# Keeping four weight tiles for the second token tile, and sending its last 512 columns out by ScalarE and an adding transfer

## The chip, the core and the metric

The kernel runs on one core of a Trainium2 chip. Its engines are TensorE (PE, with its weight loads as PEld), VectorE (DVE), ScalarE (ACT), GpSimd (POOL) and SyncE (SP). SP and POOL also issue transfers between memory and the on-chip buffers, which 16 DMA engines carry out. The metric is the device time in microseconds (us), as the median of several runs.

## The reference

One layer of a hybrid encoder on 256 tokens of width 2048, all in float32. A mixer (two kinds of attention and a recurrence) comes first; its output is normalised and added to x. Then comes the part that matters here:

```python
hdn = jnp.square(jax.nn.relu(_rms_norm(x, norm_mlp_pre[l]) @ w_mlp_up[l]))
x = x + _rms_norm(hdn @ w_mlp_down[l], norm_mlp_post[l])
```

with w_mlp_up of 2048 x 8192 and w_mlp_down of 8192 x 2048. `_rms_norm` divides a token's row by the root of the mean of its squares and multiplies by a gain for each column. The last product, its norm and the addition to x end the kernel.

## The kernel before

Each float32 weight is used as the sum of two rounded parts: ACT copies a weight tile of 128 x 1024 into the upper part (`whi`, L158), DVE subtracts to get the lower part (`wlo`, L159), and TensorE multiplies with both. The 256 tokens are two token tiles of 128 (`tt` = 0, 1). Weight tiles come from memory one by one: `wraw` (L143) issues a load on SP's queue into one of three `raw` buffers, `wsplit` (L151) splits it, and `wnext` (L162) keeps one tile ahead. The parts go to three buffers each of `whi` and `wlo`, unless the list `homes` (L149) names another place for that tile; `raw2` (L1185) makes such places, of which there are six.

The residual x stays in memory (`xs`) while the large products run, and is fetched back into `x1[0]` and `x1[1]` near the end. The sums of the last product are gathered in `ys[0]` and `ys[1]`, 128 x 2048 each.

The end of the kernel is the loop at L1600. It takes the last eight 128-row blocks of `hdn` and multiplies them by four groups g of 512 columns; each group takes four weight tiles. `tok` (L192) does one group. For most weight tiles it multiplies for both token tiles (12 matmuls, L220); the last `lag` tiles are kept: they are multiplied for token tile 0 first (six matmuls each, L204), then token tile 0 is given out, then the kept tiles are multiplied for token tile 1. `lag` is 1, and 3 for g = 3.

In the group g = 2 the residual is fetched back (L1608), in four transfers of 512 KB on SP's queue. For each token tile, DVE adds the product to `ys` (L1611), ACT squares and sums (L1612), and DVE multiplies by the gain (L1615). For g = 3 the row's factor follows: `rstd_of` (L1158) takes the mean on DVE (L1166) and raises it to the power -0.5 on POOL (L1167). `final` (L1623) then scales a piece of columns, adds the residual (DVE, L1625) and issues its transfer to the output (SP, L1626). For token tile 0, two pieces of 512 columns are done so and two more after the last addition of token tile 1 (L1638, L1639); for token tile 1 it is three pieces of 512 columns and two of 256.

A planner arranges the instructions of each engine, and of each queue, when the program is built. It goes by when their inputs and buffers come free in its own reckoning, and then by program order. The matmuls of this part are planned like the rest. `issue_after` puts an instruction behind another on the same engine. On the chip each engine and each queue runs its list in order: an instruction that waits holds up all behind it. POOL can issue transfers that add to what is at their destination (`accum_op`, L1439); before, these add weight tiles on the chip.

Of the kernel before, what the change touches and what calls it, by code (L numbers as in the profile page):

```python
# [12 lines left out]
AF = mybir.ActivationFunctionType  # L13
ALU = mybir.AluOpType
# [36 lines left out]
def hybrid_block(ctx, tc, xt, x, gains, params, consts, lora, gup, wst, out):  # L51
    nc = tc.nc
    V, A, G, PE = nc.vector, nc.scalar, nc.gpsimd, nc.tensor
# [11 lines left out]
    def nm(s):  # L65
        uid[0] += 1
        return f"{s}_{uid[0]}"

    def gps():
        return pg.tile([128, 512], F32, tag="gps", name=nm("gps"), bufs=4)  # L70
# [54 lines left out]
    def tick(us):  # L125

        clock[0] += us
        while any([step(th) for th in list(threads)]):
            pass
# [19 lines left out]
    homes = []  # L149
# [12 lines left out]
    def wnext():  # L162

        while len(wq) < 1 + AHEAD and (order or wpos[0] < wst.shape[0]):
            wsplit(wraw(order.pop(0) if order else None))
            if side:
                side.pop(0)()
        return wq.pop(0)
# [15 lines left out]
    def unit(pks):  # L184

        ps = gps()
        for h in range(2):
            hi, lo = wnext()
            gemm(ps, hi, lo, pks[8 * h:8 * h + 8], h == 0, h == 1, tick)
        return ps  # L190

    def tok(pks, lag=1):  # L192


        ps = [gps(), gps()]
        n = len(pks)
        kept = []

        def prod(hl, k0, tt):
            for w, parts in ((hl[0], (0, T)), (hl[1], (0,))):  # L200
                for k in (k0, k0 + 1):
                    for part in parts:
                        c = part + tt * 128
                        PE.matmul(ps[tt], pks[k][:, c:c + 128], w[:, (k - k0) * 512:(k - k0) * 512 + 512],  # L204
                                  start=k == 0 and part == 0 and w is hl[0], stop=w is hl[1] and k == n - 1)
                    if k == k0 + 1 or w is hl[0]:
                        tick(2 * US)

        for k0 in range(0, n, 2):
            hl = wnext()  # L210
            if k0 >= n - 2 * lag:
                prod(hl, k0, 0)
                kept.append((hl, k0))
                continue
            for w, parts in ((hl[0], (0, T)), (hl[1], (0,))):
                for k in (k0, k0 + 1):
                    for tt in range(2):
                        for part in parts:
                            c = part + tt * 128
                            PE.matmul(ps[tt], pks[k][:, c:c + 128], w[:, (k - k0) * 512:(k - k0) * 512 + 512],  # L220
                                      start=k == 0 and part == 0 and w is hl[0], stop=False)
                        tick(len(parts) * US)
        yield ps[0]
        for hl, k0 in kept:
            prod(hl, k0, 1)
        yield ps[1]
# [91 lines left out]
    w = {}  # L318
# [92 lines left out]
    for h in range(8):  # L411
        ps = qb[h] if h < 3 else unit(upk)
# [641 lines left out]
    for s in ("q", "k"):  # L1054
        lst = []
        for h in range(4):
            ps = unit(upk)
# [12 lines left out]
    for hf in range(2):  # L1070
        for s, mo in (("k", MU_K), ("r", MU_R), ("v", MU_V)):
            for p in range(4 * hf, 4 * hf + 4):
                ps = unit(upk)
# [84 lines left out]
    def rstd_of(ss, eps, sums):  # L1158

        if sums is None:  # L1160
            sums = cpool.tile([128, 1], F32, name=nm("ssum"))
            V.tensor_reduce(sums, ss[:, 0:3], AX.X, ALU.add)
            V.tensor_scalar(sums, sums, 1.0 / D, eps, ALU.mult, ALU.add)
            return sums
        r = cpool.tile([128, 1], F32, name=nm("rs"))
        V.tensor_scalar(r, ss[:, 3:4], 1.0 / D, sums, ALU.mult, ALU.add)  # L1166
        G.tensor_tensor(r, r, cst[:, 2:3], ALU.pow)  # L1167
        return r

    g2, loads = gain(0, [fm().rearrange("p a b -> p (a b)")[:, 0:512] for _ in range(4)])  # L1170
    x1 = [p2.tile([128, D], F32, tag="x1", name=nm("x1"), bufs=2) for _ in range(2)]
    for c in range(0, D, 512):
        for tt in range(2):
            loads.append(lambda tt=tt, c=c: nc.sync.dma_start(out=x1[tt][:, c:c + 512],
                                                              in_=x[tt * 128:tt * 128 + 128, c:c + 512]))
# [3 lines left out]
    def junk():  # L1179
        return p2.tile([128, 512], F32, tag="junk", name=nm("junk"), bufs=2)  # L1180
# [10 lines left out]
    for g in range(4):  # L1191
# [4 lines left out]
        for tt, ps in enumerate(tok(mpk, 5 if g == 3 else 1)):  # L1196
            def gained():
                return V.tensor_tensor(mg[tt][:, gs], ps, g2[g], ALU.mult)
# [148 lines left out]
    ys = []  # L1347
    hid, fmh, fml, hp = {}, {}, {}, {}
# [176 lines left out]
    for j in range(2):  # L1525
        up(j)
        ps, post = heads[j]
# [69 lines left out]
    hp = [hp[k] for k in range(FIRST[4], FIRST[4] + SIZES[4])]  # L1597
    g4, loads = gain(1, [pk() for _ in range(4)])
    side.extend(loads)
    for g in range(4):  # L1600
        gs = slice(512 * g, 512 * g + 512)
        if g == 2:
            assert not threads
            spare.clear()
            x1 = [p2.tile([128, D], F32, tag="x1", name=nm("x1"), bufs=2) for _ in range(2)]
            for tt in range(2):
                for c in (0, 1024):
                    nc.sync.dma_start(out=x1[tt][:, c:c + 1024], in_=xs[tt][:, c:c + 1024])  # L1608
        for tt, ps in enumerate(tok(hp, 3 if g == 3 else 1)):
            yv = ys[tt][:, gs]  # L1610
            added = V.tensor_tensor(yv, yv, ps, ALU.add)  # L1611
            A.activation(junk(), yv, AF.Square, accum_out=ss4[:, tt, g:g + 1])  # L1612

            def gained():
                V.tensor_tensor(yv, yv, g4[g], ALU.mult)  # L1615

            if g < 3:
                gained()
                if g == 2:
                    sum4.append(rstd_of(ss4[:, tt, :], eps4[tt], None))  # L1620
                continue

            def final(c, w):  # L1623
                cs = slice(c, c + w)
                V.scalar_tensor_tensor(x1[tt][:, cs], ys[tt][:, cs], r4, x1[tt][:, cs], ALU.mult, ALU.add)  # L1625
                nc.sync.dma_start(out=out[tt * 128:tt * 128 + 128, cs], in_=x1[tt][:, cs])  # L1626

            if tt == 0:
                r4 = rstd_of(ss4[:, 0, :], None, sum4[0])
                gained()  # L1630
                final(0, 512)
                final(512, 512)
                r40 = r4
                continue
            with tc.issue_after(added.ins):
                for c in (1024, 1536):
                    cs = slice(c, c + 512)
                    V.scalar_tensor_tensor(x1[0][:, cs], ys[0][:, cs], r40, x1[0][:, cs], ALU.mult, ALU.add)  # L1638
                    nc.sync.dma_start(out=out[0:128, cs], in_=x1[0][:, cs])  # L1639
            r4 = rstd_of(ss4[:, 1, :], None, sum4[1])  # L1640
            gained()
            for c, w in ((0, 512), (512, 512), (1024, 512), (1536, 256), (1792, 256)):
                final(c, w)


# [123 lines left out]
```

## Time and profile before

| | us |
|---|---|
| median of 3 runs | 1495.91 (1495.70 to 1497.13) |
| the profiled execution, its time | 1496.71 |
| the profiled execution, its span | 1494.9 |
| TensorE busy | 1480.5 |
| TensorE's granted clock, mean | 0.998 |

The span runs from the first to the last instruction. Times in the views are microseconds from the start of the span. Busy time of one instruction includes what overlaps with the next one on the same engine, so that matmuls of 0.39 us follow each other more closely than that. The column of a wait names what ended last before the instruction could start.

### The profile page before, as it was taken

The page shows a single profiled execution, that of the slowest core. Times are in us where ns is not written, and L with a number is a line of the kernel's source. Part 1 is how long each engine was busy: PE and PEld are TensorE (multiplying, and loading weights), DVE is VectorE, ACT ScalarE, POOL GpSimd, SP SyncE. Part 2 cuts the span into 40 slices and gives each one's busy share as a digit, 9 for nine tenths or more (in the row PEclk, how much of TensorE's full clock was granted, in tenths as well). Part 3 has the DMA queues.
Part 4 walks back from the last instruction along what each step waited for, and adds up shares of the span by engine and source line. Part 5 has one row for each costly group of instructions (what it writes and reads, how often), then busy time and mean ns, then how long its engine had stood idle before and what let it go on. Part 6 is the DMA issues. An engine that isn't in the chain of part 4 may idle for free.

```text
span 1494.9 us, 22860 instructions
## 1 busy us (share of the span) xinstructions
PE 1480.5 (99%) x8429; PEld 1250.2 (84%) x8429; DVE 1214.0 (81%) x1688; ACT 933.9 (62%) x1396; POOL 91.3 (6%) x160
## 2 busy tenths in 40 slices
PE   9999999999999999999999999999999999999997
PEld 7888888888778888788888888888888888888885
DVE  7576677899679798567646788999899999899986
ACT  7465666664576554574445767776766677677653
POOL 0021000100001100000000000000000000000000
PEclk9999999999999999999999999999999999999999
DMA  7545545445544556445755768888888888889874
GB/s 274 187 152 189 169 169 179 171 165 192 175 150 167 179 172 201 152 148 197 267 197 202 277 213 246 258 257 257 242 254 245 262 240 249 258 246 280 261 248 155
DMA packets 107759, 317.70 MB, mean 213 GB/s; under 512 B 10752, under 2 KB 14976, under 8 KB 107392
## 3 DMA queue, kind: packets, MB, share of 16 engines
q1 hardware_dynamic: 94400, 283.34, 55.2%
q0 software_dynamic: 8064, 29.36, 10.5%
q10 hardware_dynamic: 5184, 3.54, 0.8%
q8 instruction: 66, 1.08, 0.3%
q14 instruction: 45, 0.37, 0.1%
HBM read 282.65 MB, written 4.19 MB: 192 GB/s over the span
## 4 chain that ended last, share of the span: by engine, by line
PE 96%; DVE 1%; ACT 1%; issue 1%; POOL 0%; DMA 0%; POOLq 0%; DVEq 0%; ACTq 0%; SPq 0%
PE gps L220 28%; PE gps L174 22%; PE gps L178 13%; PE gps L204 7%; PE mps L1479 3%; PE mps L1477 3%; PE mps L1478 3%; PE gps L1479 3%; PE gps L1477 2%; PE gps L1478 2%; PE gps L182 2%; PE gps L335 1%; PE mps L790 1%; DVE wlo L159 0%; PE gps L1236 0%
## 5 line engine op out<-in xcount | busy, mean ns | idle before, releaser
L159 DVE TENSOR_TENSOR wlo<-raw,whi 128x1024 fp32r<-128x1024 f32 x497 | 602.3, 1220 | 154.0 <-ACT whi L158 139.5
L158 ACT ACTIVATE whi<-raw 128x1024 fp32r<-128x1024 f32 x497 | 522.7, 1056 | 247.9 <-PE gps L220 85.4
L174 PE MATMUL gps<-pk,whi 128*128 128x512 f32 x1336 | 336.6, 391 | 0.4 <-ACT whi L158 0.4
L174 PEld LDWEIGHTS gps<-pk,whi 128*128 128x128 f32 x1336 | 247.3, 188 | 48.9 <-ACT whi L158 0.6
L220 PE MATMUL gps<-whi,pk 128*128 128x512 f32 x1136 | 286.0, 391 | 0.0
L220 PEld LDWEIGHTS gps<-whi,pk 128*128 128x128 f32 x1136 | 211.5, 188 | 44.0
L178 PEld LDWEIGHTS gps<-pk,wlo 128*128 128x128 f32 x1424 | 194.1, 190 | 14.1 <-DVE wlo L159 0.3
L178 PE MATMUL gps<-pk,wlo 128*128 128x256 f32 x1424 | 199.2, 282 | 0.0
L220 PE MATMUL gps<-wlo,pk 128*128 128x512 f32 x568 | 155.2, 392 | 0.0
L220 PEld LDWEIGHTS gps<-wlo,pk 128*128 128x128 f32 x568 | 105.6, 188 | 21.9
L1340 DVE TENSOR_TENSOR sp<-raw,sp 128x1024 fp32r<-128x1024 f32 x67 | 81.7, 1219 | 3.4 <-ACT sp L1339 3.1
L1368 ACT ACTIVATE sp<-gps 128x512 f32<-128x512 f32 x52 | 31.1, 598 | 80.0 <-PE gps L182 80.0
L1339 ACT ACTIVATE sp<-raw 128x1024 fp32r<-128x1024 f32 x67 | 70.6, 1054 | 14.0 <-PE mps L1478 4.9
L204 PE MATMUL gps<-whi,pk 128*128 128x512 f32 x256 | 68.9, 390 | 0.0
L1477 PE MATMUL mps<-whi,fm 128*128 128x512 f32 x168 | 66.2, 394 | 0.0
L1478 PE MATMUL mps<-whi,fm 128*128 128x512 f32 x168 | 65.8, 392 | 0.0
L1479 PE MATMUL mps<-wlo,fm 128*128 128x512 f32 x168 | 65.6, 391 | 0.1
L1439 POOL DMA_DIRECT2D raw<-raw x40 | 34.9, 874 | 426.2 <-DVE raw L1436 110.1
L204 PEld LDWEIGHTS gps<-whi,pk 128*128 128x128 f32 x256 | 47.7, 188 | 9.9
L1479 PE MATMUL gps<-wlo,fm 128*128 128x512 f32 x126 | 49.3, 391 | 0.5 <-DVE wlo L159 0.5
L1477 PE MATMUL gps<-whi,fm 128*128 128x512 f32 x126 | 49.2, 391 | 0.0
L1436 DVE TENSOR_TENSOR raw<-raw,raw 128x1024 f32<-128x1024 f32 x40 | 48.8, 1219 | 0.4
(393 smaller groups left out, 2007.2 us busy)
## 6 DMA issues: line engine op xcount, KB each, us to landing
raw<-in_wst_dram SPq DMA_DIRECT2D x499, 512.0 KB, 4.4
raw<-raw POOLq DMA_DIRECT2D x40, 512.0 KB, 7.1
sp<-in_wst_dram SPq DMA_DIRECT2D x16, 512.0 KB, 5.7
raw<-sp POOLq DMA_DIRECT2D x8, 512.0 KB, 6.4
sp<-raw POOLq DMA_DIRECT2D x8, 512.0 KB, 7.3
x<-in_x_dram SPq DMA_DIRECT2D x8, 256.0 KB, 5.6
xs<-x SPq DMA_DIRECT2D x2, 1024.0 KB, 4.6
x<-xs SPq DMA_DIRECT2D x4, 512.0 KB, 6.9
```

Of the source, the lines that this page charges most:

```text
L158: A.activation(hi, raw, AF.Copy)
L159: V.tensor_tensor(lo, raw, hi.bitcast(F32), ALU.subtract)
L174: PE.matmul(ps, hi[:, i * 128:i * 128 + 128], pks[i], start=first and i == 0, stop=False)
L178: PE.matmul(ps[:, 0:T], lo[:, i * 128:i * 128 + 128], pks[i][:, 0:T], start=False, stop=False)
L204: PE.matmul(ps[tt], pks[k][:, c:c + 128], w[:, (k - k0) * 512:(k - k0) * 512 + 512], start=k == 0 and part == 0 and w is hl[0], stop=w is ...
L220: PE.matmul(ps[tt], pks[k][:, c:c + 128], w[:, (k - k0) * 512:(k - k0) * 512 + 512], start=k == 0 and part == 0 and w is hl[0], stop=False)
L1339: A.activation(hi, raw, AF.Copy)
L1340: V.tensor_tensor(lo, raw, hi.bitcast(F32), ALU.subtract)
L1436: V.tensor_tensor(x, x, z, ALU.add)
L1477: PE.matmul(Q[f], p, w, start=d == 0 and i == 0, stop=False)
L1478: PE.matmul(Q[f], pl, w, start=False, stop=False)
L1479: PE.matmul(Q[f], p, wl, start=False, stop=d == nd - 1 and i == 1)
```

## The change

For g = 3, `tok` keeps all four weight tiles (`lag` 4), and the parts of the fourth go to a pair of `raw2` buffers. Token tile 0 does three pieces of 512 columns before, and one after, the last addition of token tile 1. For token tile 1 the columns 1536 to 2047 are taken from DVE and SP: in the block of g = 2 the residual of these columns is copied from `x1[1]` to the output in memory (a transfer of 256 KB on SP's queue), and at the end ACT multiplies `ys[1]` there by the row's factor into `x1[1]`, and POOL issues a transfer that adds this to the output in memory. DVE and SP do the other columns in pieces of 512, 512, 256 and 256.

```diff
                 for c in (0, 1024):
                     nc.sync.dma_start(out=x1[tt][:, c:c + 1024], in_=xs[tt][:, c:c + 1024])
-        for tt, ps in enumerate(tok(hp, 3 if g == 3 else 1)):
+            nc.sync.dma_start(out=out[128:256, 1536:2048], in_=x1[1][:, 1536:2048])
+        if g == 3:
+            homes[:] = [None, None, raw2]
+        for tt, ps in enumerate(tok(hp, 4 if g == 3 else 1)):
...
                 r4 = rstd_of(ss4[:, 0, :], None, sum4[0])
                 gained()
-                final(0, 512)
-                final(512, 512)
+                for c in (0, 512, 1024):
+                    final(c, 512)
                 r40 = r4
                 continue
             with tc.issue_after(added.ins):
-                for c in (1024, 1536):
+                for c in (1536,):
                     cs = slice(c, c + 512)
...
             r4 = rstd_of(ss4[:, 1, :], None, sum4[1])
             gained()
-            for c, w in ((0, 512), (512, 512), (1024, 512), (1536, 256), (1792, 256)):
+            part = x1[1][:, 1536:2048]
+            A.activation(part, ys[1][:, 1536:2048], AF.Copy, scale=r4)
+            G.dma_start(out=out[128:256, 1536:2048], in_=part, accum_op=ALU.add)
+            for c, w in ((0, 512), (512, 512), (1024, 256), (1280, 256)):
                 final(c, w)
```

## Rows read from the trace of the kernel before

**Rows 1.** The page, busy us of each engine, share of the span, instructions.
```profile
PE 1480.5 (99%) x8429; PEld 1250.2 (84%) x8429; DVE 1214.0 (81%) x1688; ACT 933.9 (62%) x1396; POOL 91.3 (6%) x160
```

**Rows 2.** Chain of waits from 1440 on, pieces of g = 3: start, us, what.
```profile
1473.97 2.72 PE gps L220 x12
1476.69 4.09 PE gps L204 x18
```

**Rows 3.** DVE in order of time: start, us, engine, line, output<-inputs, count, idle before.
```profile
1483.61 1.42 DVE L1625 SCALAR_TENSOR_TENSOR x<-y,rs,x 128x512 f32<-128x512 f32 x2 [0.46 <-POOL rs L1167]
1484.95 0.68 DVE L1611 TENSOR_TENSOR y<-y,gps 128x512 f32<-128x512 f32 x1
1485.54 1.41 DVE L1638 SCALAR_TENSOR_TENSOR x<-y,rs,x 128x512 f32<-128x512 f32 x2
1486.87 0.20 DVE L1166 TENSOR_SCALAR rs<-ss,ssum 128x1 f32<-128x1 f32 x1
...
1488.11 2.87 DVE L1625 SCALAR_TENSOR_TENSOR x<-y,rs,x 128x512 f32<-128x512 f32 x5 [0.44 <-POOL rs L1167]
```

**Rows 4.** ACT and POOL in order of time, the same stretch.
```profile
1485.72 0.63 ACT L1612 ACTIVATE junk<-y 128x512 f32<-128x512 f32 x1 [3.41 <-DVE y L1611]
1486.25 0.19 ACT L1612 ACTIVATION_READ_ACCUMULATOR junk<-y 128x1 f32 x1
...
1487.15 0.92 POOL L1167 TENSOR_TENSOR rs<-rs,cst 128x1 f32<-128x1 f32 x1 [3.57 <-DVE rs L1166]
```

**Rows 5.** Line L1626: landing of all seven writes; then the last one alone.
```profile
DMA to landing us min/median/max: 2.5/2.8/3.2
...
L1626 SPq DMA_DIRECT2D out_dram<-x x1: 411/411/411, 1491.1 to 1491.1; - x1
DMA to landing us min/median/max: 2.9/2.9/2.9
```

**Rows 6.** DVE and ACT in order of time: splits of the last two weight tiles.
```profile
1475.28 1.22 DVE L159 TENSOR_TENSOR wlo<-raw,whi 128x1024 fp32r<-128x1024 f32 x1
1475.87 1.06 ACT L158 ACTIVATE whi<-raw 128x1024 fp32r<-128x1024 f32 x1 [0.21 <-ACT junk L1612]
1477.20 1.21 DVE L159 TENSOR_TENSOR wlo<-raw,whi 128x1024 fp32r<-128x1024 f32 x1
```

**Rows 7.** Groups by line and form: count | busy us, mean ns | idle before.
```profile
L1091 ACT ACTIVATE th<-gps,rt 128x512 f32<-128x512 f32 x22 | 14.8, 679 | 7.5 <-PE gps L204 5.9 <-DVE wlo L159 1.5
```

**Rows 8.** Line L1439, adding transfers: landing of all 56; then the last alone.
```profile
DMA to landing us min/median/max: 4.5/7.0/11.0
...
DMA to landing us min/median/max: 5.1/5.1/5.1
```

**Rows 9.** DMA queues (packets, MB, share) from 1431 to 1438.5; 1488.6 to 1494.9; 1486.2 to 1488.6.
```profile
q0 software_dynamic: 144, 0.52, 35.3%
...
q1 hardware_dynamic: 734, 1.06, 54.0%
...
q1 hardware_dynamic: 365, 0.67, 80.3%
```

**Rows 10.** SP's queue and ACT in time; landing of L1608, of L145; SP's longest wait.
```profile
1441.50 2.08 SPq L1608 DMA_DIRECT2D x<-xs  x2
1444.94 0.33 SPq L145 DMA_DIRECT2D raw<-in_wst_dram  x1
1449.00 1.55 SPq L145 DMA_DIRECT2D raw<-in_wst_dram  x2
...
1453.42 1.06 ACT L158 ACTIVATE whi<-raw 128x1024 fp32r<-128x1024 f32 x1 [0.69 <-DMA raw<-in_wst_dram]
...
DMA to landing us min/median/max: 4.0/6.9/8.3
...
DMA to landing us min/median/max: 3.1/4.4/7.1
...
SPq L1608 <- DMA raw<-sp: 5.6, 1, 5.6
```

## The prediction

> **What bounds the kernel now.** I read the page's busy times first, then the chain of waits, then the last stretch in order of time, then the queues. TensorE is busy for 1480.5 us, 99% of the span [rows 1]. So whatever the change does beside a running TensorE is worth nothing, unless it makes TensorE wait. Only the stretch after the last matmul can become shorter.
>
> In the chain of waits the last column group (g = 3) starts at 1473.97: 12 matmuls that serve both token tiles (2.72 us), then 18 for the first token tile, 18 for the second [rows 2]. One matmul steps 2.72/12 = 0.227 us. The first token tile is complete at 1476.69 + 4.09 = 1480.78, the second at 1473.97 + 48 x 0.227 = 1484.85. From there to the end of the span, 1494.9, there are 10.05 us without a matmul: this tail is all that the change works on directly.
>
> The tail in order of time [rows 3, 4]: DVE adds the last product (L1611, 1484.95), ACT squares and sums (L1612, 1485.72, its sum is read out until 1486.25 + 0.19 = 1486.44), DVE makes the mean (L1166) only at 1486.87, POOL raises it to the power -0.5 (L1167, 1487.15), DVE scales and adds five pieces (L1625, from 1488.11), and SP sends each to memory. The last transfer is issued at 1491.1 and lands 2.9 us later [rows 5], at 1494.0; 0.9 us of closing follow. Two things stand out. For the first token tile the same chain took 1483.61 - 1480.78 = 2.83 us from its last matmul to its first scaled piece [rows 2, 3]; for the second it took 1488.11 - 1484.85 = 3.26. The difference, 0.43 us, is DVE still doing two pieces of the first tile (L1638, 1485.54 to 1486.95) when ACT's sum is there at 1486.44. And the five pieces and their issue take 1491.1 - 1488.11 = 3.0 us, one engine doing them all.
>
> **The change, part by part.** (1) *Four weight tiles kept instead of three.* The number of matmuls is the same, 48, so TensorE still ends at 1484.85, but the first 24 are all for the first token tile: it is complete at 1473.97 + 5.44 = 1479.41, that is 1.37 us sooner. In return the weight tiles are wanted sooner, the third at 1476.69 instead of 1478.05, the fourth at 1478.05 (upper parts) and 1478.05 + 4 x 0.227 = 1478.96 (lower parts) instead of 1479.41 and later. By the rows their splits are there in time: the third's lower part is done at 1475.28 + 1.22 = 1476.50, the fourth's upper part at 1475.87 + 1.06 = 1476.93, and its lower part at 1477.20 + 1.21 = 1478.41, 0.55 us ahead [rows 6]. The fourth goes to a pair of other buffers (raw2), so that it no longer waits for the first to be used up. Cost taken: 0. If DVE orders something else ahead, one 512-column operation (0.68 us) costs 0.1 us of TensorE.
>
> (2) *Three pieces of the first tile ahead of the last product, one behind.* They can start at 1479.41 + 2.83 = 1482.24 and take 3 x 0.71 = 2.1 us of DVE [rows 3], until 1484.4, before the last product at 1484.85. Behind it one piece is left, until about 1486.3, ahead of ACT's sum. So the 0.43 us are gained: the first scaled piece of the second tile comes at 1484.85 + 2.83 = 1487.68.
>
> (3) *The last 512 columns leave DVE and SP.* DVE and SP then do 512, 512, 256 and 256 columns. One 512 step is 0.67 us (half of 1.41, less the overlap; 2.87 for all five) [rows 3], so SP's last issue comes at 1491.1 - 0.43 - 0.67 = 1490.0, and with the same 2.9 us of landing and 0.9 of closing this branch ends at 1493.8: **1.1 us** ahead of before. This is the most that the tail can give.
>
> (4) *The new branch.* ACT scales 512 columns with a factor for each partition: 0.63 us by L1612, 0.68 by the nearest row with such a factor, L1091 [rows 4, 7]. It starts at 1487.68 like DVE, since both wait for the same power, so POOL can issue the adding transfer at about 1488.4. POOL has nothing else to do. What the transfer takes to land, the trace of before shows only for others: 512 KB into SBUF, 4.5 / 7.0 / 11.0 us (least, median, most), and 5.1 for the last one, which ran nearly alone at its end [rows 8]. Here it is 256 KB into memory. Its packets took 35.3% of 16 engines in 7.5 us [rows 9], 42 engine-us or 2.65 us on all 16 engines; half the bytes save 1.3 us, so alone it would land in 3.8. That is the lower end, and 7.0, the median of the full size among other traffic, the upper; 11.0 is a tail. I take 4.9: the 3.8, 0.7 for the writes beside it (the tail's own writes stretch from 2.5 to 3.2 us [rows 5]), and 0.4 for a destination that no row shows. So this branch ends at 1488.4 + 4.9 + 0.9 = 1494.2, later than SP's 1493.8, and sets the end: **0.7 us** ahead of before. Each us of landing shifts this one to one; at 5.6 us nothing is gained.
>
> (5) *The copy of the residual into the output, in the g = 2 block.* It is one more transfer of 256 KB on SP's queue, ahead of weight loads, and it waits until the last load of the residual has landed. The second pair of those loads is issued from 1441.50 on, and they land up to 8.3 us later, so at 1450.4 at most [rows 10]. Behind the waiting SP stand weight loads: in the trace one at 1444.94 and two from 1449.00 to 1450.5 [rows 10]. Where the planner puts the copy, the trace doesn't show. If behind the first of these, the two others go out 1.4 to 1.9 us later. The load of 1449.00 is split at 1453.42, as soon as it lands, and done at 1454.48; it serves the third tile of g = 1, which TensorE wants at 1473.97 - 6 x 2.72 = 1457.65, six tiles of 12 matmuls before g = 3 [rows 2, 10]. The cover is 3.2 us, so nothing reaches TensorE. That SP can stand still without harm is in the trace: it waited 5.6 us for a landing just before [rows 10], at TensorE's 99%. Cost taken: 0; the other place is a rival below.
>
> **The sum.** Against the profiled execution's own span, 1494.9 becomes 1494.2, -0.7 us. Its time is 1496.71, 0.8 above the median of the runs, 1495.91; I carry the difference over to the median: 1495.91 - 0.7 = **1495.2 us**.
>
> **Rivals.**
> *A, slower: the adding transfer is late.* It decides from a landing of 5.6 us on. For it: the median of 56 such transfers is about 7.0, none was under 4.5, and memory has to be read as well as written. Against it: half the bytes, no loads beside it. At 7.0 the span ends at 1488.4 + 7.0 + 0.9 = 1496.3, the time is 1497.3. Only at 8.6 and more does it pass 0.2%, 3.0 us, which is about what a measurement of this kernel can tell from no change; the row's most, 11.0, would give 1501.3.
>
> *B: the tail is bound by the 16 DMA engines, not by who issues.* The writes in the last 6.3 us took 54.0% of the 16 engines, 54.4 engine-us for 1.06 MB. Plain 256 KB cost 12 (80.3% of 2.4 us for 0.67 MB), the adding 256 KB half of 42, so 21 [rows 9]. The tail's work grows by 9 engine-us, 0.57 us on all 16, and it starts 0.43 us sooner: +0.1 us, 1496.0. The Trainium skill ("DMA: Bandwidth & Descriptors", section "Issuing engines are not separate DMA queues") says that transfers started from different engines run on the same 16 DMA engines and interleave, and that starting them from several saves only the time of issuing; by that rule, which speaks against this change, little more than what DVE saves would be gained. Against B in the trace: the landings stretch only from 2.5 to 3.2 us, so the queue in the engines is short.
>
> *C: the copy stands directly behind the loads.* Then the weight load of 1444.94 goes out at about 1450.9 and lands 3.1 to 4.4 us later, the least and the median of the weight loads here [rows 10]; its upper part is split 1.06 us after that, at 1455.1 to 1456.4, and TensorE wants it at 1473.97 - 7 x 2.72 = 1454.93: a stall of 0.1 to 1.4 us, which nothing later gives back as TensorE is the bound. With the -0.7 of the tail: 1495.3 to 1496.6. The landings of those loads are longer than a weight load's pace, and a planner that reckons with a shorter one would put the copy early, which is for it.
>
> *D: the first tile isn't complete sooner, or its third piece is placed behind the last product.* Then (2) is gone, 0.43 us: 1495.6.
>
> **How the numbers follow.** The forecast, the tail shorter by 0.3 to 1.1 us and no stall: 50%, 1494.8 to 1495.6. A 20%, of which 4 points pass 1498.9; B 15%; C 10%; D 5%. The runs of before spread from -0.2 to +1.2 us about their median, so I put the range from 1494.4 to 1497.3: it takes in A up to the median landing, B, C and D, and leaves out A's tail and a gain for which no row speaks. The whole tail is 10 us and at most 1.1 us of it can go, so faster by over 0.2% (under 1492.9) would need something outside it: 3%. Slower by as much: A's 4 points and 2 for a larger stall of the weight stream: 6%. Within: 91%.
>
> **What would show it.** In the changed kernel's profile: the first token tile's last product added at about 1479.4 instead of 1480.8, and TensorE's last matmul 10.9 us after the start of g = 3 (a longer stretch: step 1 is wrong); one piece of the first tile between the last add and the second mean, and 2.8 us from the last matmul to the first scaled piece; ACT's scaling and POOL's issue 0.7 us behind the power; the adding transfer landing 3.8 to 5.6 us after its issue, last of all (if SP's last write lands last, step 4 was too dear; over 5.6, A); the waits of TensorE between the residual's loads and g = 2 at zero (else C). The prediction is wrong at its root if the time outside the tail moves by more than a microsecond.

## The result

The changed kernel takes 1500.48 us (median of 9 runs, 1499.39 to 1501.65) beside 1497.13 us for the kernel before, run in turn with it on the same chip (these runs lie 1.2 us above the earlier median, 1495.91): ratio 1.0023, 95% interval [1.0015, 1.0031]. It is **slower by 3.4 us**, where 0.7 us less was forecast. The profiled execution has a span of 1498.6 us. Its granted clock is 0.997, so the clock plays no part here; TensorE is busy for as long as before [rows 1]:

```profile
PE 1479.9 (99%) x8429; PEld 1250.7 (83%) x8429; DVE 1214.4 (81%) x1687; ACT 935.0 (62%) x1397; POOL 92.2 (6%) x161
```

So the loss lies in waits, at the end of the kernel. The start of the last column group (g = 3) scatters from 1473.1 to 1475.3 between the single executions of all the kernels below, and the change doesn't touch the work ahead of it, apart from one transfer. So I compare the profiles from that start on, in two parts: the **group**, from its first matmul to the first scaled piece of the second token tile, and the **tail**, from there to the end of the span. (All starts are those of the order in time, where the group of before starts at 1473.81; the chain of [rows 2] puts it 0.16 later.)

| kernel | group | tail | sum against before |
|---|---|---|---|
| before | 14.30 | 6.79 | |
| after | 15.22 | 9.23 | +3.36 |

**The group.** Before, TensorE's first and last matmuls of the group:

```profile
1473.81 1.98 PE L220 MATMUL gps<-whi,fm 128*128 128x512 f32 x8
...
1484.23 0.61 PE L204 MATMUL gps<-wlo,fm 128*128 128x512 f32 x2
```

After, in order of time: TensorE and, below it, ACT and DVE (start, us, engine, line, output<-inputs, count, idle time before it and what ended that).

```profile
1474.15 1.07 PE L204 MATMUL gps<-whi,fm 128*128 128x512 f32 x4
...
1475.52 1.07 PE L204 MATMUL gps<-whi,fm 128*128 128x512 f32 x4
1476.42 0.61 PE L204 MATMUL gps<-wlo,fm 128*128 128x512 f32 x2
1477.60 2.12 PE L204 MATMUL gps<-whi,fm 128*128 128x512 f32 x8 [0.56 <-ACT whi L158]
...
1480.23 1.52 PE L204 MATMUL gps<-w,fm 128*128 128x512 f32 x6
...
1484.53 1.52 PE L204 MATMUL gps<-w,fm 128*128 128x512 f32 x6
```

```profile
1474.31 1.06 ACT L158 ACTIVATE w<-raw 128x1024 fp32r<-128x1024 f32 x1 [2.52 <-DMA raw<-in_wst_dram]
1475.28 0.62 ACT L1615 ACTIVATE junk<-y 128x512 f32<-128x512 f32 x1
...
1475.89 0.62 ACT L1615 ACTIVATE junk<-y 128x512 f32<-128x512 f32 x1
...
1476.50 1.04 ACT L158 ACTIVATE whi<-raw 128x1024 fp32r<-128x1024 f32 x1
```

```profile
1481.79 0.69 DVE L1614 TENSOR_TENSOR y<-y,gps 128x512 f32<-128x512 f32 x1 [2.45 <-PE gps L204]
...
1484.60 2.08 DVE L1628 SCALAR_TENSOR_TENSOR x<-y,rs,x 128x512 f32<-128x512 f32 x3 [0.46 <-POOL rs L1167]
1486.59 0.68 DVE L1614 TENSOR_TENSOR y<-y,gps 128x512 f32<-128x512 f32 x1
...
1488.12 0.21 DVE L1166 TENSOR_SCALAR rs<-ss,ssum 128x1 f32<-128x1 f32 x1 [0.19 <-ACT junk L1615]
...
1489.37 2.20 DVE L1628 SCALAR_TENSOR_TENSOR x<-y,rs,x 128x512 f32<-128x512 f32 x4 [0.44 <-POOL rs L1167]
```

On ACT the tile called `w` is the fourth, in its raw2 buffer, and `whi` at 1476.50 is the third. **The fourth stands ahead of the third**: ACT stands idle for 2.52 us until the last load of all has landed, splits it, does two squares, and only then splits the third tile, done at 1477.54. In before both parts of the third were done by 1475.28 + 1.22 = 1476.50, and the fourth came behind it [rows 6]. TensorE wants the third tile 12 matmuls into the group, at 1474.15 + 12 x 0.227 = 1476.87, and starts it at 1477.60: 0.73 us lost. The eight matmuls there take 2.12 us, where eight take 1.98 in before: 0.14 us more. The planner also put five matmuls of token tile 1 among those of token tile 0, so that the first token tile is complete 7.6 us into the group, at 1480.23 + 1.52 = 1481.75, not 5.4. Its three pieces (1484.60 to 1486.68) are then still on DVE when the last matmul is done, at 1484.53 + 1.52 = 1486.05; the last addition starts 0.54 us after that, where it started 0.11 after it in before. Behind it things go as forecast: one piece, then the mean right behind ACT's sum.

| | before | after | |
|---|---|---|---|
| group's start to last matmul's end | 11.03 | 11.90 | +0.87 |
| to the last addition | 0.11 | 0.54 | +0.43 |
| to the first scaled piece | 3.16 | 2.78 | -0.38 |

**The tail.** After: POOL in order of time, then the lines of the adding transfer and of SP's last write (count: ns least/median/most, start of first and last), then those of the closing; below them the same lines of before.

```profile
1488.41 0.93 POOL L1167 TENSOR_TENSOR rs<-rs,cst 128x1 f32<-128x1 f32 x1 [3.85 <-DVE rs L1166]
1490.39 0.90 POOL L1647 DMA_DIRECT2D out_dram<-x  x1 [1.05 <-ACT x L1646]
```

```profile
L1647 POOL DMA_DIRECT2D out_dram<-x x1: 897/897/897, 1490.4 to 1490.4; - x1
...
DMA to landing us min/median/max: 5.0/5.0/5.0
...
L1629 SPq DMA_DIRECT2D out_dram<-x x1: 415/415/415, 1491.7 to 1491.7; - x1
...
DMA to landing us min/median/max: 4.4/4.4/4.4
...
L1770 POOLq DRAIN  x3: 40/93/7440, 1490.4 to 1498.3; - x3
L1770 SPq DRAIN  x3: 7/7/7, 1496.2 to 1498.1; - x3
```

```profile
L1764 POOLq DRAIN  x3: 34/93/5621, 1487.1 to 1494.7; - x3
L1764 SPq DRAIN  x3: 7/7/7, 1494.1 to 1494.4; - x3
```

The program closes with DRAINs on each engine. POOL's longest runs from the start of its last work to 1490.39 + 7.44 = 1497.83. The adding transfer lands at 1490.39 + 5.0 = 1495.4, so POOL closes **2.4 us after the landing**; 0.8 us of closing follow. SP has seen its own last write land at 1491.73 + 4.4 = 1496.1 and drains within 0.1 us, in 7 ns (1496.2); then it waits for the others. In before it is the other way round: POOL's drain ended at 1487.15 + 5.62 = 1492.8, ahead of SP's last landing [rows 5], and so it cost nothing. That the end isn't one of transfers shows in the DMA engines (1490 to 1498.6 in 40 slices, busy tenths): they are idle for the last 3 us.

```profile
DMA  0000399899899669999999542100000000000000
```

### The profile page after: what moved, and what is told of

Same layout as the page of the kernel before. It is cut to its first block, busy times and chain, and to the rows that moved or that the text cites. A ratio compares the mean times of both kernels' runs of the same rounds, so it can differ in the third digit from the quotient of the medians.

```text
span 1498.6 us, 22862 instructions
## 1 busy us (share of the span) xinstructions
PE 1479.9 (99%) x8429; PEld 1250.7 (83%) x8429; DVE 1214.4 (81%) x1687; ACT 935.0 (62%) x1397; POOL 92.2 (6%) x161
## 4 chain that ended last, share of the span: by engine, by line
PE 92%; DMA 2%; issue 2%; DVE 2%; ACT 1%; POOL 1%; SPq 0%; DVEq 0%; POOLq 0%; ACTq 0%
PE gps L220 27%; PE gps L174 22%; PE gps L178 12%; PE gps L204 7%; PE mps L1477 3%; PE mps L1478 3%; PE mps L1479 3%; PE gps L1479 2%; PE gps L1477 2%; PE gps L1478 2%; PE gps L182 1%; DMA raw<-in_wst_dram 1%; DVE wlo L159 1%; DMA raw<-raw 1%; PE mps L790 1%
## 5 line engine op out<-in xcount | busy, mean ns | idle before, releaser
L1439 POOL DMA_DIRECT2D raw<-raw x40 | 35.0, 874 | 430.1 <-DVE raw L1436 109.1
```

## The experiments

Three theories stood against each other for the tail. **W**: POOL's closing drain waits for its transfer to land and takes 2.4 us more. **A**: it is the adding that is slow, in landing and beside SP's writes; a plain transfer from POOL would cost nothing. **D**: POOL's drain takes a fixed time from its last issue on, whatever lands. For the group: the order in which the planner splits the kept tiles (**S**), or the copy of the residual (rival **C** of the prediction), with **K**, that the copy makes later weight loads slower and so uses up their cover. Where an expectation names a theory by a letter, these are meant, or those that it explains itself; A and D are not the prediction's rivals of the same letters. Where an expectation counts from the group's start, it is the chain's, 0.16 us later than in the tables here.

**1. The tail alone.** Before, with the copy, ACT's scaling and the adding transfer; three kept tiles, two pieces and two.

```diff
+            nc.sync.dma_start(out=out[128:256, 1536:2048], in_=x1[1][:, 1536:2048])
...
-            for c, w in ((0, 512), (512, 512), (1024, 512), (1536, 256), (1792, 256)):
+            part = x1[1][:, 1536:2048]
+            A.activation(part, ys[1][:, 1536:2048], AF.Copy, scale=r4)
+            G.dma_start(out=out[128:256, 1536:2048], in_=part, accum_op=ALU.add)
+            for c, w in ((0, 512), (512, 512), (1024, 256), (1280, 256)):
```

> The copy of the residual, ScalarE's scaling and POOL's adding transfer alone; the weight tiles and the first token tile's pieces as in the kernel before. Theory P (POOL's transfer and what follows it at the end are slow by themselves): TensorE doesn't wait, the first scaled piece of the second tile comes where it did before (14.1 us behind the start of the last group), and from there to the end of the span it takes 9.2 us as in the changed kernel instead of 6.8: 2.4 us slower than before. Theory L (the end was late in the changed kernel only because it began late and met other transfers): 6.1 us, 0.7 us faster than before.

Measured: 1.0021 [1.0012, 1.0030]; group 15.12, tail 9.41. The tail's loss is whole without the tiles: landing 5.3 us, and the drain of

```profile
L1768 POOLq DRAIN  x3: 40/93/7656, 1490.7 to 1498.8; - x3
```

ends at 1490.71 + 7.66 = 1498.4, again 2.4 us behind the landing. Not expected was the group's +0.82, without any kept tile more: the load of the second weight tile of the group landed late, ACT waited 3.48 us for it, until 1473.76; the additions and squares queued behind its split came late too, with them the splits of the third and fourth tile, and TensorE lost some tenths at each of these. The profiled execution took 1500.88 us, 1.2 more than the median of this kernel's runs (1499.65), so the +0.82 may belong to that execution alone. Experiments 4, 8 and 9 look at that.

**2. The tiles alone.** Before, with four kept tiles and pieces three and one; the five last pieces by DVE and SP.

```diff
+        if g == 3:
+            homes[:] = [None, None, raw2]
-        for tt, ps in enumerate(tok(hp, 3 if g == 3 else 1)):
+        for tt, ps in enumerate(tok(hp, 4 if g == 3 else 1)):
...
-                final(0, 512)
-                final(512, 512)
+                for c in (0, 512, 1024):
+                    final(c, 512)
...
-                for c in (1024, 1536):
+                for c in (1536,):
```

> Four kept weight tiles, the fourth in the other buffers, and three pieces ahead of the last addition, without the copy and the adding transfer. Theory S (the planner splits the fourth tile ahead of the third on ScalarE, and ScalarE then waits for the fourth's load): TensorE waits about 0.7 us inside the last group, the last addition comes 0.6 us after TensorE's last matmul, 0.4 us are gained at the mean, and the tail of five pieces is that of before: 0.9 us slower. Theory C (the copy on SP's queue made the loads late): no wait of TensorE, 0.4 us faster.

Measured: 1.0013 [1.0004, 1.0023]; group 15.52 (+1.22, where S expected 0.9), tail 6.81, that of before. The group's loss comes with the tiles, by the same two rows, ACT's wait for the fourth tile's load and TensorE's for the third tile:

```profile
1475.43 1.06 ACT L158 ACTIVATE w<-raw 128x1024 fp32r<-128x1024 f32 x1 [2.83 <-DMA raw<-in_wst_dram]
...
1478.71 2.11 PE L204 MATMUL gps<-whi,fm 128*128 128x512 f32 x8 [0.86 <-ACT whi L158]
```

**3. The third tile in raw2 instead of the fourth.** After, with one word moved. All else is left, the number of tiles kept too. (The list names the places of tiles two to four.)

```diff
-            homes[:] = [None, None, raw2]
+            homes[:] = [None, raw2, None]
```

> The changed kernel with one word moved: the third weight tile of the last group goes to the other buffers instead of the fourth, so that the tiles are split in the order of their loads. Theory S: no wait of TensorE in the last group, the first token tile complete 5.4 us after the group's start, the last addition right behind the last matmul: 1.4 to 1.8 us faster than the changed kernel, and still about 2 us slower than before by the tail. Theory C: as slow as the changed kernel.

Measured: 1.0017 [1.0007, 1.0027]; group 13.87, tail 9.42. Now the planner splits the tiles in the order of their loads, TensorE waits for nothing, and the group is 0.43 us shorter than in before, which is what the prediction's step (2) said (against after, 1.35 us, where S expected 1.4 to 1.8):

```profile
1473.79 1.06 ACT L158 ACTIVATE w<-raw 128x1024 fp32r<-128x1024 f32 x1
1475.09 1.06 ACT L158 ACTIVATE whi<-raw 128x1024 fp32r<-128x1024 f32 x1 [0.23 <-DMA raw<-in_wst_dram]
...
1476.93 1.52 PE L204 MATMUL gps<-w,fm 128*128 128x512 f32 x6
```

So the loss of the group is the order of two splits, not the kept tiles. The profiles show it; the intervals of the runs of after and of this one overlap.

**4. The copy alone.** Before, with the copy in the g = 2 block; the last pieces are written over it.

```diff
                     nc.sync.dma_start(out=x1[tt][:, c:c + 1024], in_=xs[tt][:, c:c + 1024])
+            nc.sync.dma_start(out=out[128:256, 1536:2048], in_=x1[1][:, 1536:2048])
```

> The kernel before with the copy of the residual into the output added in the g = 2 block and nothing else (the later pieces overwrite it). Theory S and P: no change, TensorE waits nowhere from the copy to the end. Theory C: TensorE waits 0.5 us or more in the last two groups and the span is as much longer.

Measured: 1.0004 [0.9994, 1.0013]; group 14.32, tail 7.25. No cost that can be told from none, so C is not where the 3.4 us went. The tail is 0.46 us longer with no change in its work. The lines of SP's closing tell why: in the stretch from the landing of the last write to the first two DRAINs SP has eight semaphore waits here (first row), one in before (second row).

```profile
L1765 SPq EVENT_SEMAPHORE  x8: 27/28/28, 1495.0 to 1495.4; - x8
L1764 SPq EVENT_SEMAPHORE  x1: 28/28/28, 1494.0 to 1494.0; - x1
```

SP closes with a list of waits, one after the other 0.06 us apart where nothing is left to wait for. In before the wait that the last write ends is the last of them; here seven stand behind it, 0.4 us. Experiment 8 has five behind it, 0.3 us.

**5. A plain transfer from POOL.** Before, but the last 512 columns, summed by DVE as ever, are sent by POOL.

```diff
-            for c, w in ((0, 512), (512, 512), (1024, 512), (1536, 256), (1792, 256)):
+            cs = slice(1536, 2048)
+            V.scalar_tensor_tensor(x1[1][:, cs], ys[1][:, cs], r4, x1[1][:, cs], ALU.mult, ALU.add)
+            G.dma_start(out=out[128:256, cs], in_=x1[1][:, cs])
+            for c, w in ((0, 512), (512, 512), (1024, 256), (1280, 256)):
```

> The kernel before, with the write of the last 512 columns issued by POOL instead of SP, as a plain write of the finished sum (DVE does all five pieces, no copy, no adding). POOL can issue it about 1.4 us behind the first scaled piece. Theory D (POOL's closing drain takes a fixed 6.6 us from the end of the last transfer's issue on): the drain ends 8.9 us behind the first scaled piece, the span 2.9 us longer than before. Theory W (the drain ends 2.4 us after the transfer has landed): a plain write lands about 3.4 us after its issue, so 1.2 us longer than before. Theory A (only the adding is slow, the drain is not a cost of its own): SP's last writes set the end, no change.

Measured: 1.0007 [0.9998, 1.0017]; group 14.31, tail 7.83 (+1.04). The transfer, its landing and the drain:

```profile
L1644 POOL DMA_DIRECT2D out_dram<-x x1: 620/620/620, 1489.1 to 1489.1; - x1
...
DMA to landing us min/median/max: 2.9/2.9/2.9
...
L1767 POOLq DRAIN  x3: 40/102/5374, 1489.1 to 1494.9; - x3
```

Landed at 1492.0, drained at 1489.09 + 5.37 = 1494.5: 2.5 us later, and 0.8 us behind SP, which drains at 1493.7. By the profile a plain transfer from POOL sets the end too, so A falls as the whole cause; the runs can't tell this kernel from before. D falls: the drain was 5.4 us from the issue here, 7.4 to 7.7 with the adding transfer. This run alone doesn't show W, though. The drain ended 4.7 to 4.8 us after POOL's last work (1489.09 + 0.62), and in before, with no transfer to land, it was 4.7 (1487.15 + 0.92 to 1492.8). That the landing counts is seen where the drain is longer than that: 6.5 and 6.8 us in after and experiment 1, with landings of 5.0 and 5.3, and 10.3 in experiment 7. The landings also give the price of the adding: 256 KB land in 5.0 to 5.3 us with it, 2.9 without.

**6. The tiles in the order of their loads, alone.** Experiment 2 with the word of experiment 3: `homes[:] = [None, raw2, None]`.

> Four kept weight tiles with the third in the other buffers, three pieces of the first token tile ahead of the last addition, and the tail of before: five pieces by DVE and SP, no copy, no POOL transfer. Theory S: TensorE doesn't wait in the last group, the first scaled piece of the second tile comes 13.7 us behind the group's start instead of 14.1, the tail is 6.8 us: 0.4 us faster than before. If the early split of the tiles isn't what made the changed kernel's last group late, TensorE waits 0.7 us again and it is 0.9 us slower.

Measured: 1.0003 [0.9995, 1.0012]; group 13.87, tail 6.83. The profile has the 0.4 us gained; the runs can't tell it from nothing.

**7. A tiny transfer from POOL.** Before, and POOL also sends the 128 row factors (4 bytes for each partition) to a scratch place in memory that nobody reads, just behind the power.

```diff
+            G.dma_start(out=dp.tile([128, 1], F32, name=nm("rd")), in_=r4)
             for c, w in ((0, 512), (512, 512), (1024, 512), (1536, 256), (1792, 256)):
```

> The kernel before, and behind the second power one more transfer from POOL: 128 rows of 4 bytes, plain, into a scratch place in memory. Theory D (a fixed 6.6 us after the issue): POOL's drain ends 7.5 us behind the first scaled piece, the span is 1.5 us longer than before. Theory W (2.4 us after the landing): the transfer lands 2 to 3 us after its issue, the drain ends ahead of SP's last landing, no change. Theory A: no change.

Measured: 1.0042 [1.0028, 1.0056]; group 14.31, tail 12.14. The expectation under W was that it costs nothing, since so few bytes would land early. They took 8.5 us to land, longer than the adding transfers:

```profile
L1642 POOL DMA_DIRECT2D rd<-rs x1: 618/618/618, 1489.8 to 1489.8; - x1
...
DMA to landing us min/median/max: 8.5/8.5/8.5
...
L1765 POOLq DRAIN  x3: 40/93/10867, 1489.8 to 1501.5; - x3
...
L1626 SPq DMA_DIRECT2D out_dram<-x x5: 332/332/413, 1490.3 to 1492.6; - x5
...
DMA to landing us min/median/max: 7.7/8.1/8.6
```

The number expected was wrong, the mechanism not: landed at 1498.3, drained at 1489.82 + 10.87 = 1500.7, 2.4 us later, whatever lands. SP's five writes beside it took 7.7 to 8.6 us instead of 2.5 to 3.2 [rows 5], though, so here SP's branch closes last (it drains at 1500.9) and the time isn't the drain's.

**8. Three copies.** Before, with copies of three pieces of 512 columns in the g = 2 block, all written over at the end.

```diff
+            nc.sync.dma_start(out=out[128:256, 1536:2048], in_=x1[1][:, 1536:2048])
+            nc.sync.dma_start(out=out[128:256, 1024:1536], in_=x1[1][:, 1024:1536])
+            nc.sync.dma_start(out=out[128:256, 512:1024], in_=x1[1][:, 512:1024])
```

> The kernel before with three times the suspected copy: 1536 residual columns of the second token tile copied into the output in the g = 2 block (three writes of 256 KB on SP's queue in the same place), nothing else. Theory K (the copy makes later weight loads land late, as seen in three of the four kernels with it: 5.2 to 5.4 us instead of 3.3 to 3.7 for the load about 7 us ahead of the last group): late loads again, and with three copies the weight loads behind SP's wait another 1 us, so TensorE waits in the last two groups, 0.5 to 1.5 us slower than before. Theory N (those landings are scatter of the single execution): no wait of TensorE, within 0.5 us of before.

Measured: 1.0008 [0.9998, 1.0018]; group 15.46, tail 7.07. TensorE loses 1.16 us in the group, with a wait row like that of experiment 1 (PE for DVE's lower part, 0.3 us), behind a weight load that was issued at 1469.4 and landed in 5.3 us. Over all the kernels, the third-last weight load, that of the group's second tile, landed in 5.2 to 5.4 us in four of the five that have a copy in the g = 2 block (experiments 1, 3, 4, 8; 3.5 in after), and in 3.1 to 3.7 in the seven without it or with it early. That speaks for K by count. The loss reached TensorE only in two of the four, the profiled executions of these two lie 1.2 and 1.7 us above the medians of their runs, and the runs can't tell experiments 4 and 8 from before. Why a transfer that has long landed should make a load of 512 KB slower that is issued some 17 us behind it, no row shows: that is **open**.

**9. The copy early.** Experiment 3, but the copy stands right behind the line that puts the residual away, long before the end.

```diff
     nc.sync.dma_start(out=xs[1], in_=x1[1])
+    nc.sync.dma_start(out=out[128:256, 1536:2048], in_=x1[1][:, 1536:2048])
```

> The changed kernel with the third weight tile in the other buffers and the residual's copy issued 600 us earlier, right behind the write of the residual itself, from the same buffer, so that no copy stands among the last weight loads. Theory K: the load about 7 us ahead of the last group lands in 3.3 to 3.7 us. Both: first scaled piece of the second tile 13.7 us behind the last group's start, and 9.4 us from there to the end (adding transfer 5.2, drain 2.4, closing 0.8): 2.2 us slower than before. If the tail shrinks, the copy's place had a part in it.

Measured: 1.0015 [1.0006, 1.0025]; group 13.87, tail 9.39. With tiles and copy out of the way, the tail alone still costs what it cost, +2.6 us.

**10. The adding transfer for the first token tile.** Experiment 9, but copy, ACT's scaling and the adding transfer serve the last 512 columns of token tile 0; token tile 1 goes out in its five pieces by DVE and SP, as in before.

```diff
+                part = x1[0][:, 1536:2048]
+                A.activation(part, ys[0][:, 1536:2048], AF.Copy, scale=r4)
+                G.dma_start(out=out[0:128, 1536:2048], in_=part, accum_op=ALU.add)
...
-            with tc.issue_after(added.ins):
-                for c in (1536,):
-                    cs = slice(c, c + 512)
-                    V.scalar_tensor_tensor(x1[0][:, cs], ys[0][:, cs], r40, x1[0][:, cs], ALU.mult, ALU.add)
-                    nc.sync.dma_start(out=out[0:128, cs], in_=x1[0][:, cs])
```

> The same scaling by ScalarE and the same adding transfer of 512 columns, but for the first token tile, about 4 us sooner (its residual copied early, as in the run before); the second tile's five pieces by DVE and SP as in the kernel before, the weight tiles in the order of their loads. Theory W (an adding transfer costs what its landing and the 2.4 us of drain behind it reach past SP's last landing): landing and drain end about 1.5 us ahead of SP's last landing, so first scaled piece 13.7 us behind the last group's start, 6.8 us of tail, 0.4 us faster than before. If a POOL transfer near the end costs by itself, wherever it stands, the tail is 8 us or more and it is slower than before.

Measured: 0.9997 [0.9988, 1.0006]; group 13.89, tail 6.80. The same adding transfer, 5.1 us in landing, issued 4.4 us ahead of the first scaled piece of the second tile, costs nothing:

```profile
1482.69 0.90 POOL L1638 DMA_DIRECT2D out_dram<-x  x1 [1.06 <-ACT x L1637]
```

```profile
L1764 POOLq DRAIN  x3: 40/102/5724, 1486.1 to 1493.7; - x3
```

It lands at 1487.8, 2.4 us more is 1490.2, and POOL's drain ends only 1486.14 + 5.72 = 1491.9 as it does in before, some time behind its last power; SP sets the end. By the profile this kernel is 0.4 us shorter than before, like experiment 6; neither can be told from before by its runs.

| profile of | group | tail | sum against before | measured ratio |
|---|---|---|---|---|
| after | 15.22 | 9.23 | +3.36 | 1.0023 |
| 1 tail alone | 15.12 | 9.41 | +3.44 | 1.0021 |
| 2 tiles alone | 15.52 | 6.81 | +1.24 | 1.0013 |
| 3 third tile in raw2 | 13.87 | 9.42 | +2.20 | 1.0017 |
| 4 copy alone | 14.32 | 7.25 | +0.48 | 1.0004 |
| 5 plain from POOL | 14.31 | 7.83 | +1.05 | 1.0007 |
| 6 tiles in load order | 13.87 | 6.83 | -0.39 | 1.0003 |
| 7 tiny transfer | 14.31 | 12.14 | +5.36 | 1.0042 |
| 8 three copies | 15.46 | 7.07 | +1.44 | 1.0008 |
| 9 copy early | 13.87 | 9.39 | +2.17 | 1.0015 |
| 10 adding for first tile | 13.89 | 6.80 | -0.40 | 0.9997 |

The sum from one profile and the ratio from the runs (1.0010 is 1.5 us) agree within 1 us in every row.

## Why the prediction was wrong

The span was forecast at 1494.2 and is 1498.6, 4.4 us more. By the prediction's own steps:

- **Ahead of the group**: 0.34, the scatter of its start.
- **Step (1), kept tiles, "cost taken: 0"**: failed, by 0.87. The matmuls' needs were right, and the splits as they stood in before would have been in time. But I took the order of the splits from the trace of before [rows 6], and the change itself gave the planner a reason for another one: the fourth tile's buffer in raw2 is free early, the third's has to be used up first. The price that I named for a slip, 0.1 us, was that of one DVE operation; what came was ACT's whole wait for the last load. Experiment 3 shows it, and the sign that the prediction named for this step came: the last matmul ends 11.9 us into the group, not 11.0.
- **Step (2), the pieces**: the 0.43 was right: from the last addition on 0.38 here, and 0.43 over the group in experiments 3, 6 and 9. What spoiled it was step (1): with the first tile complete at 1481.75, the three pieces run past the last matmul, +0.43. Together with the 0.05, steps (1) and (2) account for 0.87 + 0.43 + 0.05 = 1.35.
- **Step (3), SP's branch**: the issue was right, 2.36 us behind the first scaled piece (forecast 1490.0 - 1487.68 = 2.32). The landing was not: 4.4 us beside the adding transfer, taken as 2.9. This branch alone would have made the tail 2.36 + 4.4 + 0.9 = 7.7, longer than that of before; it isn't what ended last.
- **Step (4), the adding branch**: the landing, the term that I spent most on, was right (5.0, forecast 4.9), but its parts (3.8, 0.7 and 0.4) were never tested apart, so the sum may have come out by luck. The issue came 1.02 us behind the power, not 0.72: 0.72 of ACT and 0.30 from ACT to POOL. The term that failed is the **0.9 of closing**, read behind SP's last landing [rows 5] and used for POOL as well. For POOL it is 2.4 + 0.8 = 3.2. 0.3 + 0.1 + 2.3 = 2.7: the rest of the 4.4.
- **Step (5), the copy**: the planner put it one load later than I took it, behind two weight loads and not one, and SP waited 0.8 us there. Its cost is zero within what runs can tell (experiment 4), with K left open.

Of the rivals, A was decided by a landing over 5.6 us: it was 5.0, and the time is later than A's 1497.3 all the same. B, that the 16 DMA engines bind, has half of it right: SP's last 128 KB write landed in 4.4 us beside the adding transfer and in 2.9 without it. The Trainium skill ("DMA: Bandwidth & Descriptors", section "Issuing engines are not separate DMA queues") says that transfers started by different engines interleave on the same 16 DMA engines. The two landings agree with that. But the engines stand idle for the last 3 us, so it isn't they that set the end: the tail lost 2.4 us at POOL's closing, where B expected 0.1 in all. C: no stall at the residual's loads. D's first condition came true: the first token tile is complete 7.6 us into the group, later than in before (7.0), though all pieces stand where they were meant to. Its price, step (2)'s 0.43, isn't what was paid: that gain came behind the last addition, and the cost came ahead of it, as above. Slower by over 0.2%, as measured, was given 6%, all of it to A's tail and the weight stream: no rival asked what each engine does between its last transfer and the end of the program, though the row was there: in before POOL's DRAIN is 5.6 us long behind 0.92 us of work, and SP's 7 ns.

What would have made the forecast: for each engine that gets a new last instruction, read its own closing lines. From the trace of before alone the 2.4 could not be had, since POOL sends nothing near the end there; but a bound above nothing could: 5.6 us of drain behind a bare power, which is 4.7 behind its end. As an estimate, put behind POOL's issue as forecast (1488.4, with the 0.90 us that the issue took), that makes 1488.4 + 0.9 + 4.7 + 0.8 = 1494.8, and the gain over 1494.9 is all but gone.

## What to carry to other kernels

A transfer's end for the program is not its landing: it is when the engine that issued it has closed, and here that was 0.1 to 0.5 us later on SP and 2.4 us on POOL. Whatever POOL sends should be issued well ahead of the end (4.4 us before the first of the last pieces was enough), and the last bytes should be left to SP. When a change gives a tile another buffer, look at what a planner will do with a buffer that is free sooner: an earlier split of a later load holds up all that is behind it on the engine.

## What the runs showed of the hardware

- POOL's DRAIN at the end of the program ended 2.4 us after the landing of POOL's last transfer, in five profiles, for landings of 5.0 to 5.3 and 8.5 us (after, experiments 1, 3, 7 and 9). With no transfer near the end it took 5.6 to 5.7 us from the start of POOL's last power, 4.7 to 4.8 from its end. In experiment 5, with a landing of 2.9 us, both readings fit.
- SP's DRAIN came 0.1 us after the landing of SP's last write, and 0.5 and 0.4 us after it in experiments 4 and 8, where seven and five waits already met stood behind the one that this landing ends.
- An adding transfer of 256 KB into memory landed in 5.0 to 5.3 us, a plain one issued by POOL in 2.9; POOL's issue took 0.90 and 0.62 us. SP's 128 KB writes landed in 4.3 to 4.6 us beside the adding one, and in at most 3.5 beside the plain one.
- 128 writes of 4 bytes took 8.5 us to land and slowed SP's writes of 128 and 256 KB beside them from 2.5 to 3.2 us to 7.7 to 8.6. The Trainium skill ("DMA: Bandwidth & Descriptors", "Specifications") says that transfers under 512 B are done as read-modify-write; whether that is the reason no run here shows.
